# Second and third weight loads cut in halves by rows over two DMA queues in a one-core decoder layer

## The chip, the cores and the metric

The kernel runs on one core of one Trainium2 chip. The metric is device time of one launch in microseconds (us), where lower is better. Before the change the median of three runs is 292.22 us (291.61 to 293.05).

## The reference

One decoder layer on a single sequence of 256 tokens with 1024 features. One input projection feeds three groups of heads: block-sparse causal attention (with 256 tokens there is one block, so it is plain causal attention with a relative bias), a gated width-3 convolution, and a pooling mixer. Their outputs are joined, projected, and added to the input ahead of a layer norm; a gated MLP with a width-3 convolution and a second layer norm follow.

```python
h = x @ w_in
q, k, v, cb, cc, cx, pin = split(h)
attn = causal_attention(q, k, v, rel_bias)
conv = cb * causal_dwconv(cc * cx, conv_w)
pool = pool_mixer(pin, w_pool, pool_scale)
mix = concat([attn, conv, pool]) @ w_out
x = layer_norm(alpha * x + mix, ln1_g, ln1_b)
u, g = split(causal_dwconv(x @ w_up, ffn_conv_w) + ffn_conv_b)
return layer_norm(alpha * x + (u * silu(g)) @ w_down, ln2_g, ln2_b)
```

All inputs and the output are float32.

## The kernel before, in words

**Weights.** All weight matrices are streamed once from HBM through a ring of five buffers named `raw` (`RB = 5`). `load()` (line 96) issues the next loads of the list as long as a buffer is free. The first eight loads are chunks of `a_qk`, one for each block of 128 input features: 128 rows of 1280 float32, that is 256 columns of the transposed input and 1024 columns of the query and key weights, 640 KB in one piece of HBM. Chunks of 1024 KB follow for `a_v`, `a_cp`, `a_out`, `a_up` and `a_down`. Here load 1 is the first chunk, loads 2 and 3 are the second and third. Load 1 comes in two column pieces (lines 106 and 107); all other loads are one DMA each (line 104). All are issued by SyncE (SP), in list order. A load into a buffer that was used before waits until the engines have done with the old content.

**Splitting.** Matmuls run on float32 values split into two float32r numbers. `split` (line 122) takes a raw tile: ScalarE (ACT) writes the high part `hi` (line 123) and VectorE (DVE) writes the remainder `lo` (line 124). For an `a_qk` chunk, `wsplit` (line 130) first splits the 256 input columns into `xh` and `xl`, then the 1024 weight columns into `hi` and `lo`: in three pieces for load 1 (columns 0 to 255 are used unsplit), two for load 2, one for each later load.

**TensorE at the start.** 23 small matmuls on zeros (`WARM`, line 162) run while load 1 is under way. Then come the eight query and key blocks: `qk_block(0)` begins with two matmuls on the raw float32 data (line 200) and continues with 18 split products through `mm3` (line 152); each later `qk_block(k)` has 24 products of 128x256 (line 192), the first 16 of which need `xh`, `xl` and `hi` of load k + 1 and the last 8 `lo`. All eight blocks add into the same four PSUM banks, so they run in order. The value projection, attention, the other mixers, the output projection and the MLP follow, all fed from the same ring.

**Elsewhere.** GpSimd (POOL) issues `prm` and `bias` (lines 176 and 177) once load 4 has landed. ACT issues only output DMAs, at the end. `half` (line 163) is a 128x1 tile of constants that DVE fills at the start; in the kernel before, only GpSimd reads it, in the layer norms.

**Order.** Each engine runs its instructions in program order. The order is written out by hand in `trunk`: `load()` (line 696), the splits of loads 1 and 2, then the blocks with the splits of later loads between them.

Of the kernel before, what the change touches and what calls it, by code (L numbers as in the profile page):

```python
# [10 lines left out]
F32 = mybir.dt.float32  # L11
BF16 = mybir.dt.bfloat16
F32R = mybir.dt.float32r
AF = mybir.ActivationFunctionType
# [3 lines left out]
P = 128  # L18
# [17 lines left out]
LAG = 5  # L36
KEEP = 7
FIRST = 2
WARM = 23


# [16 lines left out]
def trunk(ctx, tc, a_qk, a_v, a_cp, a_out, a_up, a_down, x, par, tab, lnp, out):  # L58
    nc = tc.nc
    cp = ctx.enter_context(tc.tile_pool(name="cp", bufs=1))  # L60
# [6 lines left out]
    def bank():  # L67
        return ps.tile([P, 512], F32, name="bank")
# [14 lines left out]
    for n, i in units:  # L83
        at = {"qk": a_qk, "v": a_v, "cp": a_cp, "out": a_out, "u": a_up, "g": a_up, "d": a_down}[n]
        c = i if n in ("qk", "u", "g") else i // 2
# [3 lines left out]
    for u in units:  # L89
        at, c, _ = src_of[u]  # L90
# [3 lines left out]
    raws, left = [], {}  # L94

    def load():

        while len(raws) < len(loads) and (len(raws) < RB or not left[raws[len(raws) - RB]]):
            at, c = loads[len(raws)]
            key = id(at), c  # L100
            n = S + H if at is a_qk else 2 * H
            raw = raw_of[key] = rp.tile([P, n], F32, name="raw")
            if raws:
                nc.sync.dma_start(raw, at[c])
            else:
                nc.sync.dma_start(raw[:, :2 * S], at[c][:, :2 * S])
                nc.sync.dma_start(raw[:, 2 * S:], at[c][:, 2 * S:])
            raws.append(key)
            left[key] = 1 if at is a_qk else 2
# [7 lines left out]
    def used(u):  # L117
        at, c, _ = src_of[u]
        left[id(at), c] -= 1
        load()  # L120
# [39 lines left out]
    warm = bank()  # L160
    for i in range(WARM):
        nc.tensor.matmul(warm[:, :P], zero, zero, start=True, stop=True)
    half = cp.tile([P, 1], F32, name="half")
# [224 lines left out]
    def sum_rows(accs, rows, last, t, p, lh, ll, h, l, i):  # L388

        ts = slice(t * P, (t + 1) * P)  # L390
        if len(accs[t]) == 0:
            accs[t].extend((bank(), bank()))
        if t == 1 and p == 2 and len(accs[t]) == 2:
            accs[t].append(bank())
        whole = p is None or t == 0
        for b in range(2) if p is None else (p,):
            c, n = (b * 512, 512) if whole else PIECES[t][p]
            o = accs[t][b] if whole else accs[t][p][:, :n]
            mm3(o, lh[:, ts], ll[:, ts], h[:, c:c + n], l[:, c:c + n],
                i == 0 or (t == 1 and p == 2 and i == last), i == rows - 1, skip=True)  # L400
# [16 lines left out]
    def w_out(t, i, p):  # L417
        h, l = W["out", i]
        kt = order[i]
        sum_rows(acc, KD, FIRST, t, p, mh[:, kt], ml[:, kt], h, l, i)  # L420

# [5 lines left out]
    def w_out_last(t, p):  # L427
        for i in range(FIRST, KD):
            w_out(t, i, p)
# [144 lines left out]
    def block(pe, need=(), a=(), b=(), now=False, hold=0, more=True):  # L574
        blocks.append((pe, list(need), list(a), list(b), now, hold, more))
# [60 lines left out]

    for i in range(FIRST):
        block(L(w_out_first, i), [("out", i)])
    last = [("out", i) for i in range(FIRST, KD)]
    block(L(w_out_last, 0, 0), last, [L(rs, 0, 0)], hold=4)  # L640
# [48 lines left out]
    def ready(i):  # L689
# [3 lines left out]
        at, c, _ = src_of[splits[nsplit]]  # L693
        return (id(at), c) in raw_of

    load()
    for _ in range(2):
        wsplit()
# [85 lines left out]
```

## Time and profile before

| | |
|---|---|
| median of three runs | 292.22 us (291.61 to 293.05) |
| profiled execution, its time | 291.71 us |
| profiled execution, its span from first to last instruction | 289.6 us |
| TensorE (PE) matmul busy | 282.8 us, 98% |
| VectorE (DVE) busy | 220.9 us, 76% |
| ScalarE (ACT) busy | 158.4 us, 55% |
| GpSimd (POOL) busy | 40.6 us, 14% |
| moved by DMA | 56.21 MB, mean 194 GB/s |

The time of a run is the span and 2.1 us around it. Busy shares are means over the whole span; TensorE's matmuls overlap one another, so its 98% says that it rarely stands still, not that it runs at its best. Positions in the trace are us from the start of the span. In the trace's tables, an engine name with a q (SPq, ACTq) is that engine's own queue of DMA issues, and DMA queue q1 is the one that SyncE feeds, q0 the one that GpSimd feeds. "Idle before" is how long an engine stood idle ahead of an instruction, and the arrow names what released it. KB is 1024 bytes, MB and GB are decimal.

### The profile page before, as it was taken

What the parts mean: (1) busy time and instruction counts of PE and PEld (TensorE: products, weight loads), DVE (VectorE), ACT (ScalarE), POOL (GpSimd) and SP (SyncE); (2) the same over time, 40 slices, a digit from 0 to 9 for tenths busy, and PEclk for the clock granted to TensorE, in tenths of its full rate; (3) what the DMA queues carried; (4) which work ended last, traced back from release to release, by engine and by line L of the source; (5) the groups of instructions that cost most, each with busy time, mean ns of one, the idle gap of its engine ahead of it and who ended that gap; (6) DMA issues with size and microseconds to landing.
All of it is one profiled execution on the core that took longest, in us unless ns stands there. A gap on an engine that the chain in (4) does not pass through costs nothing.

```text
span 289.6 us, 5052 instructions
## 1 busy us (share of the span) xinstructions
PE 282.8 (98%) x2040; PEld 262.8 (91%) x2040; DVE 220.9 (76%) x384; ACT 158.4 (55%) x263; POOL 40.6 (14%) x42
## 2 busy tenths in 40 slices
PE   8899999999999999999999999999999999999993
PEld 7899779999878999999999999999999999999891
DVE  2774756797958699998988888888667777668584
ACT  3754675828412394366766666666555665655100
POOL 0300004950000289800000000000000000000010
PEclk9999999999999999999999999999999999999998
DMA  6999974143990169284737374848474462200022
GB/s 252 378 354 407 414 272 148 18 145 134 361 359 2 62 231 377 74 285 149 278 147 290 148 285 149 291 148 292 145 290 147 174 224 81 102 2 0 0 76 72
DMA packets 9447, 56.21 MB, mean 194 GB/s; under 512 B 1040, under 2 KB 1552, under 8 KB 3792
## 3 DMA queue, kind: packets, MB, share of 16 engines
q1 hardware_dynamic: 7920, 50.86, 47.1%
q0 software_dynamic: 1072, 4.51, 4.3%
q10 hardware_dynamic: 432, 0.52, 0.5%
q8 instruction: 16, 0.26, 0.4%
q14 instruction: 7, 0.06, 0.1%
HBM read 54.84 MB, written 1.05 MB: 193 GB/s over the span
## 4 chain that ended last, share of the span: by engine, by line
PE 94%; DMA 2%; DVE 1%; ACT 0%; SPq 0%; issue 0%; DVEq 0%
PE bank L152 81%; PE bank L192 7%; PE bank L485 2%; DMA raw<-a_qk 2%; PE bank L267 1%; PE bank L258 1%; PE bank L445 1%; PE bank L227 1%; PE bank L225 0%; DVE xr L565 0%; PE bank L334 0%; DVE xr L560 0%; ACT hi L123 0%; DVE stat L372 0%; DVE xr L385 0%
## 5 line engine op out<-in xcount | busy, mean ns | idle before, releaser
L124 DVE TENSOR_TENSOR lo<-raw,hi 128x1024 fp32r<-128x1024 f32 (+2 forms) x95 | 113.5, 1206 | 24.6 <-ACT hi L123 24.5
L152 PE MATMUL bank<-xh,hi 128*128 128x256 f32 x406 | 114.9, 283 | 0.0
L152 PE MATMUL bank<-xl,hi 128*128 128x256 f32 x406 | 113.6, 280 | 0.0
L152 PE MATMUL bank<-xh,lo 128*128 128x256 f32 x406 | 113.5, 280 | 0.0
L123 ACT ACTIVATE hi<-raw 128x1024 fp32r<-128x1024 f32 (+2 forms) x95 | 95.4, 1019 | 5.2 <-DMA raw<-a_v 4.6
L152 PEld LDWEIGHTS bank<-xh,hi 128*128 128x128 f32 x406 | 76.7, 189 | 1.4 <-issue 0.7
L152 PEld LDWEIGHTS bank<-xl,hi 128*128 128x128 f32 x406 | 76.8, 189 | 0.8
L152 PEld LDWEIGHTS bank<-xh,lo 128*128 128x128 f32 x406 | 76.7, 189 | 0.0
L152 PE MATMUL bank<-hi,mh 128*128 128x512 f32 (+1 forms) x133 | 49.4, 372 | 0.0
L152 PE MATMUL bank<-lo,mh 128*128 128x512 f32 (+1 forms) x133 | 49.2, 370 | 0.0
L152 PE MATMUL bank<-hi,ml 128*128 128x512 f32 (+1 forms) x133 | 49.0, 369 | 0.0
L496 ACT ACTIVATE y<-bank,prm 128x256 f32<-128x256 f32 x44 | 24.6, 560 | 25.8 <-PE bank L152 13.6
L152 PEld LDWEIGHTS bank<-hi,ml 128*128 128x128 f32 x133 | 25.1, 188 | 4.5 <-DVE ml L124 0.2
L410 POOL TENSOR_TENSOR mv<-mv,half 128x1 f32<-128x1 f32 x4 | 2.8, 699 | 186.2 <-DVE mv L409 186.2
L152 PEld LDWEIGHTS bank<-hi,mh 128*128 128x128 f32 x133 | 25.1, 189 | 4.1 <-ACT mh L123 0.4
L152 PEld LDWEIGHTS bank<-lo,mh 128*128 128x128 f32 x133 | 25.1, 188 | 3.5
L497 DVE SCALAR_TENSOR_TENSOR y<-bank,prm,y 128x255 f32<-128x255 f32 x44 | 21.0, 478 | 8.7 <-ACT y L496 8.6
L123 ACT ACTIVATE mh<-f 128x256 fp32r<-128x256 f32 x22 | 9.2, 418 | 24.3 <-DVE f L506 24.3
L498 DVE SCALAR_TENSOR_TENSOR y<-bank,prm,y 128x254 f32<-128x254 f32 x44 | 21.2, 482 | 1.6
L124 DVE TENSOR_TENSOR ml<-f,mh 128x256 fp32r<-128x256 f32 x22 | 11.0, 500 | 10.6 <-ACT mh L123 10.6
L502 ACT ACTIVATE sg<-y 128x256 f32<-128x256 f32 x22 | 9.2, 419 | 13.8 <-DVE y L498 13.8
L192 PE MATMUL bank<-xh,hi 128*128 128x256 f32 x56 | 13.6, 281 | 0.9 <-ACT hi L123 0.9
(105 smaller groups left out, 265.9 us busy)
## 6 DMA issues: line engine op xcount, KB each, us to landing
raw<-a_up SPq DMA_DIRECT2D x22, 1024.0 KB, 4.8
raw<-a_down SPq DMA_DIRECT2D x11, 1024.0 KB, 5.9
raw<-a_qk SPq DMA_DIRECT2D x7, 640.0 KB, 7.8
raw<-a_cp SPq DMA_DIRECT2D x4, 1024.0 KB, 12.7
raw<-a_out SPq DMA_DIRECT2D x4, 1024.0 KB, 4.8
raw<-a_v SPq DMA_DIRECT2D x2, 1024.0 KB, 10.5
lnp<-lnp POOLq DMA_DIRECT2D x4, 512.0 KB, 4.7
bias<-tab POOLq DMA_DIRECT2D x1, 1024.0 KB, 13.3
```

Source lines behind the costliest of these rows:

```text
L123: nc.scalar.activation(hi, raw, AF.Copy)
L124: nc.vector.tensor_sub(lo, raw, hi.bitcast(F32))
L152: nc.tensor.matmul(o, l, r, start=start and i == 0, stop=stop and i == 2, skip_group_check=skip)
L192: nc.tensor.matmul(o, (l if low else h)[:, ws], r[:, k, :], start=False, stop=low and k == KD - 1, skip_group_check=True)
L227: nc.tensor.matmul(s_ps[h][:, P:P + S], qT[r, j, 1], kT[r, j], start=True, stop=True)
L258: nc.tensor.transpose(t_ps[:, i * P:(i + 1) * P], pr[:, i * P:(i + 1) * P], ident)
L267: nc.tensor.matmul(o_ps[s * DH:(s + 1) * DH, t * P:S], v[:, t, h * DH:(h + 1) * DH], pts[h][:, t * S:S + t * P], start=t == 0, stop=t == N ...
L485: nc.tensor.matmul(u_ps[0][:, c:c + P], part(("ug"[s], 0))[:, k * P:(k + 1) * P], xf[:, k, t * P:(t + 1) * P], start=t == 0 and n == 0, st ...
L496: nc.scalar.activation(y, src, AF.Identity, scale=w[2], bias=prm[:, C_FB + c:C_FB + c + 1])
L497: nc.vector.scalar_tensor_tensor(y[:, 1:], src[:, :S - 1], w[1], y[:, 1:], op0=ALU.mult, op1=ALU.add)
L498: nc.vector.scalar_tensor_tensor(y[:, 2:], src[:, :S - 2], w[0], y[:, 2:], op0=ALU.mult, op1=ALU.add)
L502: nc.scalar.activation(ys[j, 2], ys.pop((j, 1)), AF.Silu)
```

## The change

Loads 2 and 3 (`BOTH = 2`) are each issued as two DMAs of 64 rows: rows 0 to 63 by SyncE, rows 64 to 127 by ScalarE. Ahead of the first `load()`, ScalarE runs a new one-column Copy (`first <- half`); the load of the activation table, which stands ahead of the first activation of a program, thereby stands ahead of ScalarE's two DMA issues.

```diff
--- before.py
+++ after.py
@@ -36,6 +36,7 @@
 LAG = 5
 KEEP = 7
 FIRST = 2
+BOTH = 2
 WARM = 23
 
 
@@ -100,7 +101,11 @@
             key = id(at), c
             n = S + H if at is a_qk else 2 * H
             raw = raw_of[key] = rp.tile([P, n], F32, name="raw")
-            if raws:
+            if 0 < len(raws) <= BOTH:
+
+                nc.sync.dma_start(raw[:P // 2], at[c][:P // 2])
+                nc.scalar.dma_start(raw[P // 2:], at[c][P // 2:])
+            elif raws:
                 nc.sync.dma_start(raw, at[c])
             else:
                 nc.sync.dma_start(raw[:, :2 * S], at[c][:, :2 * S])
@@ -693,6 +698,9 @@
         at, c, _ = src_of[splits[nsplit]]
         return (id(at), c) in raw_of
 
+
+    first = cp.tile([P, 1], F32, name="first")
+    nc.scalar.activation(first, half, AF.Copy)
     load()
     for _ in range(2):
         wsplit()
```

Lines of code behind the added ones have higher numbers in the changed program: line 123 becomes 128, 104 becomes 109, 106 becomes 111.

ScalarE's queue from its start, before (`raw_120` is load 1, `raw_123` load 2, `raw_125` load 3, `raw_127` load 4, `raw_129` load 5; a DMAHW semaphore counts a landed DMA):

```order
L123 ACT_TABLE_LOAD
L123 ACTIVATE xh_74<-raw_120 128x256 [waits DMAHW0_49]
L123 ACTIVATE hi_133<-raw_120 128x256 [waits DMAHW1_49]
L123 ACTIVATE hi_133<-raw_120 128x256 x2
L123 ACTIVATE xh_74<-raw_123 128x256 [waits DMAHW2_49]
L123 ACTIVATE hi_143<-raw_123 128x512 x2
L123 ACTIVATE xh_74<-raw_125 128x256 [waits DMAHW3_49]
L123 ACTIVATE hi_178<-raw_125 128x1024
L123 ACTIVATE xh_74<-raw_127 128x256 [waits DMAHW4_49]
L123 ACTIVATE hi_186<-raw_127 128x1024
```

and with the change (`raw_122` is load 1, `raw_125` load 2, `raw_128` load 3, `raw_131` load 4, `raw_133` load 5):

```order
L703 ACT_TABLE_LOAD
L703 ACTIVATE first_120<-half_102 128x1 [waits DVE_49]
L107 DMA raw_125<-a_qk 64x1280
L107 DMA raw_128<-a_qk 64x1280
L128 ACTIVATE xh_74<-raw_122 128x256 [waits DMAHW0_49]
L128 ACTIVATE hi_137<-raw_122 128x256 [waits DMAHW1_49]
L128 ACTIVATE hi_137<-raw_122 128x256 x2
L128 ACTIVATE xh_74<-raw_125 128x256 [waits DMAHW3_49,DMAHW2_49]
L128 ACTIVATE hi_147<-raw_125 128x512 x2
L128 ACTIVATE xh_74<-raw_128 128x256 [waits DMAHW5_49,DMAHW4_49]
L128 ACTIVATE hi_182<-raw_128 128x1024
L128 ACTIVATE xh_74<-raw_131 128x256 [waits DMAHW6_49]
```

The table load keeps its place at the head. The one-column Copy and two DMA issues stand between it and the first split, and the first instruction on load 2, and that on load 3, waits for two landings in place of one.

SyncE's queue from its start, before (names as above; `raw_172` and `raw_174` are loads 6 and 7):

```order
L106 DMA raw_120<-a_qk 128x512
L107 DMA raw_120<-a_qk 128x768
L104 DMA raw_123<-a_qk 128x1280
L104 DMA raw_125<-a_qk 128x1280
L104 DMA raw_127<-a_qk 128x1280
L104 DMA raw_129<-a_qk 128x1280
L104 DMA raw_172<-a_qk 128x1280 [waits DMAHW0_49,DMAHW1_49,DVE_49,PE_49]
L104 DMA raw_174<-a_qk 128x1280 [waits DMAHW2_49,DVE_49]
```

and with the change (`raw_176` and `raw_178` are loads 6 and 7):

```order
L111 DMA raw_122<-a_qk 128x512
L112 DMA raw_122<-a_qk 128x768
L106 DMA raw_125<-a_qk 64x1280
L106 DMA raw_128<-a_qk 64x1280
L109 DMA raw_131<-a_qk 128x1280
L109 DMA raw_133<-a_qk 128x1280
L109 DMA raw_176<-a_qk 128x1280 [waits DMAHW0_49,DMAHW1_49,DVE_49,PE_49]
L109 DMA raw_178<-a_qk 128x1280 [waits DMAHW3_49,DMAHW2_49,DVE_49]
```

SyncE still issues six DMAs ahead of its first wait, in the same places; the third and fourth have 64 rows in place of 128. Loads 4 and 5 stay whole and behind them.

## Rows read from the trace of the kernel before

**Rows 1.** The page: the span, and TensorE's busy time, share and instructions.
```profile
span 289.6 us, 5052 instructions
PE 282.8 (98%) x2040; PEld 262.8 (91%) x2040; DVE 220.9 (76%) x384; ACT 158.4 (55%) x263; POOL 40.6 (14%) x42
```

**Rows 2.** The chain that ended last: start us, us, what.
```profile
1.64 6.70 DMA raw<-a_qk
...
9.35 20.05 PE bank L192 x168
```

**Rows 3.** Timeline of TensorE's matmuls, 3 to 10 us: start us, us, instruction.
```profile
3.55 2.08 PE L200 MATMUL bank<-raw 128*128 128x256 f32 x4
5.07 0.78 PE L152 MATMUL bank<-xh,hi 128*128 128x256 f32 x1
5.64 0.41 PE L152 MATMUL bank<-xl,hi 128*128 128x256 f32 x1
5.85 0.41 PE L152 MATMUL bank<-xh,lo 128*128 128x256 f32 x1
...
6.92 0.36 PE L152 MATMUL bank<-xl,hi 128*128 128x256 f32 x1
...
8.17 0.27 PE L152 MATMUL bank<-xh,lo 128*128 128x256 f32 x1
9.35 0.38 PE L192 MATMUL bank<-xh,hi 128*128 128x256 f32 x1 [0.90 <-ACT hi L123]
9.57 0.28 PE L192 MATMUL bank<-xl,hi 128*128 128x256 f32 x1
```

**Rows 4.** Timeline of ScalarE, 0 to 11 us.
```profile
0.74 1.28 ACT L123 ACT_TABLE_LOAD   x1 [0.74 <-PEq L773]
3.53 0.42 ACT L123 ACTIVATE xh<-raw 128x256 fp32r<-128x256 f32 x1 [1.51 <-DMA raw<-a_qk]
4.49 1.03 ACT L123 ACTIVATE hi<-raw 128x256 fp32r<-128x256 f32 x3 [0.54 <-DMA raw<-a_qk]
8.36 0.42 ACT L123 ACTIVATE xh<-raw 128x256 fp32r<-128x256 f32 x1 [2.84 <-DMA raw<-a_qk]
...
10.30 1.04 ACT L123 ACTIVATE hi<-raw 128x1024 fp32r<-128x1024 f32 x1
```

**Rows 5.** Timeline of SyncE's DMA issues, 0 to 3.6 us.
```profile
0.74 0.37 SPq L106 DMA_DIRECT2D raw<-a_qk  x1
1.17 0.42 SPq L107 DMA_DIRECT2D raw<-a_qk  x1
1.64 1.85 SPq L104 DMA_DIRECT2D raw<-a_qk  x4
```

**Rows 6.** All engines by stretch: A:B us, then busy, PEclk, DMA share, GB/s last.
```profile
0.00:1.74 1.74, 0.75 (x8) 0.75 (x9) 0.12 (x2) 1.00 (x1) 0.20 (x4) 1.00 0.00 0
...
2.50:4.50 2.00, 2.00 (x13) 1.70 (x12) 0.43 (x1) 0.42 (x2) 0.00 (x0) 1.00 0.97 382
4.50:8.35 3.85, 3.85 (x21) 3.50 (x19) 1.09 (x3) 1.02 (x3) 0.00 (x0) 1.00 0.96 355
...
16.00:20.00 4.00, 4.00 (x36) 4.00 (x36) 3.03 (x5) 2.04 (x5) 0.00 (x0) 1.00 0.91 340
20.00:24.00 4.00, 4.00 (x36) 4.00 (x36) 1.45 (x2) 1.01 (x2) 0.00 (x0) 1.00 1.04 399
```

**Rows 7.** DMA from 0 to 8.35 us: packets and bytes moved.
```profile
DMA packets 626, 2.24 MB, mean 268 GB/s; under 512 B 61, under 2 KB 61, under 8 KB 626
```

**Rows 8.** DMA queues from 16 to 20 us: packets, MB, share of 16 engines.
```profile
q0 software_dynamic: 173, 0.69, 48.6%
q1 hardware_dynamic: 111, 0.66, 42.7%
```

**Rows 9.** Groups by line and shape on ScalarE: its shortest; and line 566's DMA issues.
```profile
L240 ACT ACTIVATION_READ_ACCUMULATOR pr<-lg,st 128x1 f32 x16 | 3.0, 188 | 0.0
...
L566 ACTq DMA_DIRECT2D out<-xr x2: 338/338/338, 285.7 to 286.5; - x2
```

## The prediction, made before the changed kernel was run

> **What bounds the kernel now.** I read the page first: TensorE has work under way in 98% of a span of 289.6 us [rows 1], so only a stretch in which it stands still, or runs at its lower clock, has time to give. The chain of waits says where. It is TensorE nearly to its end, but at the start it runs through one transfer: load 2, issued at 1.64 us and 6.70 us under way [rows 2]. From 9.35 us the seven later query and key blocks follow without a gap, 168 matmuls in 20.05 us, 0.119 us each [rows 2].
>
> The timeline of TensorE shows the hole [rows 3]. The last matmul of block 0 starts at 8.17 and, at 0.12 us a matmul, hands over at 8.29. The first of block 1 starts at 9.35. So 1.06 us are lost, and that is all that an earlier load 2 can give back: 0.36% of the run. The profiled run took 291.71 us, 0.51 us below the median of 292.22. About 0.5%, 1.46 us, is what a measurement of this kernel can tell from no change; the three runs lie 0.5% apart. So even the full gain stays below that bound.
>
> ScalarE's timeline shows what the hole waits for: it takes up load 2 at 8.36 [rows 4], and TensorE starts 0.99 us later, after the splits of the input columns and of half the weights. TensorE would be free at 8.29, so load 2 would have to land by 7.3 us to close the hole.
>
> Is load 2 late because it is issued late? No. SyncE issues it at 1.64 us, about 0.47 us after the piece ahead of it, and all six issues are over by 3.49 [rows 5]. The first bytes move at about 1.74 us, 1.0 us after the first issue [rows 5, 6]. From 2.5 us the 16 engines are busy for 0.96 to 0.97 of the time, at 382 and then 355 GB/s [rows 6]. By 8.35 us 2.24 MB have moved [rows 7], while loads 1 and 2 together are 1280 KB, 1.31 MB. So 0.93 MB of later loads came in ahead of load 2's last byte. As SyncE issued them in order, I read this as engines out of step: most are past load 2, and a few that lag hold its last rows. In step it would have been in much sooner: up to 4.5 us 2.24 - 3.85 x 0.355 = 0.87 MB had moved, the missing 0.44 MB take 1.24 us at 355 GB/s, to 5.74. By the same count load 1's 0.66 MB had moved at 3.94, and ScalarE could take its second piece at 4.49 [rows 4], a tail of 0.55 us. With it load 2 would be in at 6.3. The lag is thus about 2.0 us, and issuing from a second queue does not obviously touch it.
>
> **The change part by part.**
>
> *The table load.* It costs nothing: it stays at 0.74 us, for 1.28 us [rows 4], while ScalarE has no input. The number of table loads stays as it is, since the one-column Copy is of the function that the splits use.
>
> *The Copy and the two issues on ScalarE.* The Copy needs `half`, which VectorE writes at the start, while the table loads; it starts at 2.02. Its price lies between nothing and 0.40 us; the nearest row is ScalarE's shortest instruction with 188 ns [rows 9], and I take 0.2. An issue costs 0.34 us on ScalarE's queue at the end [rows 9] and 0.42 to 0.47 on SyncE's at the start [rows 5]; I take 0.45. So load 2's half is issued at 2.2 to 2.3, load 3's at 2.7, and ScalarE is free at 3.1 to 3.3. Its first split starts at 3.53 [rows 4], so 0.2 to 0.4 us of waiting cover all of it. Without that cover the first split would be late by the excess.
>
> *SyncE.* Two issues shrink to half the rows, none goes away: 0.85 us before, between 0.65 and 0.85 us now, all hidden, since the engines have a backlog from 2.5 us on. Loads 4 to 6 are queued behind the same bytes as before, less what travels on the other queue; each needs the sum of all that went ahead, which is the same. GpSimd's issues, which wait for load 4, do not move. Load 6 waits for block 0 and may be issued 0.3 us later, with loads 4 and 5 still queued ahead of it.
>
> *Load 1's second piece.* Here is a cost that the diff does not show. ScalarE's halves, issued at 2.2, are with the engines about 1.0 us later, at 3.25. By then 0.87 - 1.25 x 0.382 = 0.39 MB have moved; of load 1's 0.66 MB 0.27 are missing, all of the second piece, in rows of 3 KB. If the engines take rows of the two queues in turn, each waits for one of 5 KB: 0.44 MB extra, 1.1 us at 382 GB/s. The lower end is nothing, if ScalarE's rows come only behind. I take 0.8, near the upper end: the one stretch with two busy queues, 16 to 20 us, has them moving 0.69 and 0.66 MB side by side [rows 8]. Not all of it is felt. The first split of this piece ends at 4.49 + 0.42 = 4.91 [rows 4], but the matmuls on it flow from 5.42: the second starts at 5.64, at a spacing of 0.21 [rows 3]. So 0.5 us are free and 0.3 show; block 0 ends at 8.3 to 8.6.
>
> *Load 2.* Its halves share the engines with each other, but SyncE's half now also with load 3's half on ScalarE's queue, 0.33 MB that used to come later. That is 0.92 us at 355 GB/s. Does the second queue take the lag away? Two queues together moved 340 GB/s at 16 to 20 us, one alone 399 at 20 to 24 [rows 6], so I see no sign that a second queue adds bandwidth (the GpSimd rows there are shorter, so this is a bound, not a proof). Ends: without any lag load 2 lands at 6.3 + 0.92 = 7.2, just before the 7.3 that closes the hole; change -1.06 to -0.75 us, by whether block 0 is late. With lagging engines that keep their pace over the extra rows (8 rows of load 2 to an engine from 4.49 to 8.34, so four more in 1.9), it lands at 10.2: +1.9 us. Between them lie the full lag, +0.9, and half of it, 8.34 + 0.92 - 1.0 = 8.26, -0.1. I take the middle of these two, **+0.4 us**.
>
> *Load 3.* Its bytes are the sum of all ahead of it, as before. Its split ends at 11.34 [rows 4], and block 2 would start at 9.75 + 2.83 = 12.6. No new wait there.
>
> *Sum.* 0 + 0 + 0.4, with block 0's 0.3 hidden under the later load 2: 291.71 + 0.4 = 292.1 us for the profiled execution. Beside the median of 292.22 that is **292.6 us**: no change that can be told.
>
> **The rivals.**
>
> *The halves change nothing.* The row shows 16 engines already 0.96 busy on one queue [rows 6]; if two queues only share them and the order of bytes is nearly kept, load 2 lands within 0.2 us of 8.34, and the time is 292.0 to 292.4. The Trainium skill speaks against the change in the same way: the page DMA: Bandwidth & Descriptors, section Rules for kernel authors, says of two transfers to disjoint partition halves "Don't bother — they serialize", as both spread over the same 16 engines. By that rule the sum is zero, and no run here has yet tried it. Against this rival: load 3's half moves ahead of a part of load 2.
>
> *The hole closes.* If an engine that is held up on one queue's row goes on with the other's, the lag goes, load 2 lands by 7.3 and the gain is 0.75 to 1.06 us: 291.2 to 291.5. For it: the lag is of single engines, as the 0.93 MB ahead of it show. Against it: the busy share of 0.96 leaves little idle time to fill.
>
> *TensorE falls to its lower clock.* Spacing tells the level: 0.21 us a matmul up to 6.92 us (the 1.2 GHz level), 0.119 later (2.4 GHz) [rows 2, 3]; the granted clock in the table of stretches reads 1.00 in both. The rise came after 5.9 us of unbroken work. The hole of 1.06 us did not undo it: the second matmul of block 1 takes 0.28 us [rows 3]. If load 1's piece is late enough to break the work ahead of the rise, or load 2 comes so late that the hole is much longer than this one, the level may be low again in block 1. Place: blocks 0 and 1. Price: each matmul at the lower level costs 0.09 us more, 2.2 us for a block of 24; with 1 to 1.9 us of waiting that is 3.2 to 4.1 us, 295.4 to 296.3, and less if the low stretch is short. It decides where load 2 lands after some 9.3 us, which doubles the hole. Against it: block 0 feels only 0.3 us.
>
> *The change doesn't do what it says.* If ScalarE's issues come after 3.5 us, its halves land last and also push the first split back by as much. That is a slower run, by 0.5 to 1.5 us, within the range.
>
> **How the numbers follow.** Forecast (load 2 lands between 8.2 and 10.2): 0.42. Nothing changes: 0.18. The hole closes: 0.25. Lower clock: 0.12. Late issues: 0.03. Slower by over 1.46 us needs most of the clock case (0.11) or the far end of the forecast (0.05): 0.16. Faster by over 1.46 us is more than the hole holds; 0.04 is left for the scatter of the runs. Within: 0.80. The range goes from the full gain, 292.22 - 1.06, rounded down to 291.0, to the upper end of load 2, 292.22 + 1.9 = 294.1; it leaves out most of the clock case and some scatter.
>
> **What would show it.** Right: ScalarE's two issues between 2.2 and 3.2 us and its first split still at 3.5; the split of load 1's second piece at about 5.3 in place of 4.49; ScalarE takes up load 2 at about 8.8, and block 1 starts at about 9.75; from there 0.119 us a matmul and the same distance to the end. Wrong: load 2 taken up by 7.5 (the hole closes), a second piece that is not late, a block 1 with a spacing of 0.21, or a difference that arises after 32 us, where I see no effect.

## The result, and the profile after

The changed kernel took **299.25 us** (median; 298.59 to 301.05) against 292.22 for the kernel before: a ratio of **1.0265, interval 1.0237 to 1.0293**, so 7.0 us slower by the medians and 7.7 by the ratio. The forecast was 292.6 us, in a range of 291.0 to 294.1. The profiled execution is the fastest of the changed kernel's five, 298.59 us with a span of 296.4; its account below is thus of the smallest loss that was seen.

The page of after: span, and TensorE's busy time, share and instructions.

```profile
span 296.4 us, 5057 instructions
PE 288.7 (97%) x2040; PEld 267.0 (90%) x2040; DVE 221.3 (75%) x384; ACT 159.1 (54%) x264; POOL 40.0 (14%) x42
```

The number of matmuls is unchanged, and they are busy for 288.7 us instead of 282.8 [rows 1]. Of 6.8 us more span, 5.9 are TensorE working longer on the same work, not waiting longer. The chain of after (start us, us, what) and then a row of the chain of before that wasn't shown yet say where:

```profile
1.65 8.04 DMA raw<-a_qk
...
9.78 0.42 ACT xh L128
...
10.77 21.08 PE bank L197 x168
...
107.23 182.34 PE bank L157 x1293
```

```profile
104.48 178.21 PE bank L152 x1293
```

The account, with [rows 2] for the before:

| Stretch | before | after | difference |
|---|---|---|---|
| block 1 opens at | 9.35 | 10.77 | +1.42 |
| 168 matmuls of blocks 1 to 7 | 20.05 | 21.08 | +1.03 |
| from their end to the last 1293 | 75.08 | 75.38 | +0.30 |
| last 1293 matmuls | 178.21 | 182.34 | +4.13 |

These make 6.9 of the 6.8 us; the tail is 0.1 us shorter. So there are two losses. One is at the start. The other, which is the larger, lies from 107 us on, where loads 2 and 3 have been in for some 95 us: every matmul is a little slower there.

**The late loss.** Timelines of TensorE, some 115 us into the span (start us, duration us, instruction), of before and then of after:

```profile
115.53 0.28 PE L152 MATMUL bank<-xh,hi 128*128 128x256 f32 x1
...
116.58 0.28 PE L152 MATMUL bank<-xh,hi 128*128 128x256 f32 x1
```

```profile
115.34 0.28 PE L157 MATMUL bank<-xh,hi 128*128 128x256 f32 x1
...
116.42 0.28 PE L157 MATMUL bank<-xh,hi 128*128 128x256 f32 x1
```

Both pairs are nine matmuls apart: 1.05 us before, 1.08 after, that is 0.1167 and 0.120 us each. The view of one source line from 108 to 282 us shows it in the durations (min/median/max ns, first and last start), before and after:

```profile
L152 PEld LDWEIGHTS bank<-xl,hi x326: 187/188/189, 107.8 to 264.2; 128*128 128x128 f32 x163
L152 PE MATMUL bank<-xl,hi x326: 277/279/280, 107.9 to 264.3; 128*128 128x256 f32 x163
```

```profile
L157 PE MATMUL bank<-xl,hi x334: 278/283/283, 107.9 to 271.0; 128*128 128x256 f32 x167
...
L157 PEld LDWEIGHTS bank<-xl,hi x333: 187/192/192, 108.1 to 270.8; 128*128 128x128 f32 x167
```

Weight loads take 192 ns in place of 188, matmuls 283 in place of 279, and nothing waits. The clock is not it: in the page's row of 40 slices the granted clock is 0.9 or more in every one but the second.

**The start.** ScalarE's timeline of after, then SyncE's:

```profile
0.74 1.28 ACT L703 ACT_TABLE_LOAD   x1 [0.74 <-PEq L781]
1.00 1.22 ACTq L107 DMA_DIRECT2D raw<-a_qk  x2
2.03 0.20 ACT L703 ACTIVATE first<-half 128x1 f32<-128x1 f32 x1
3.77 0.42 ACT L128 ACTIVATE xh<-raw 128x256 fp32r<-128x256 f32 x1 [1.53 <-DMA raw<-a_qk]
6.80 1.03 ACT L128 ACTIVATE hi<-raw 128x256 fp32r<-128x256 f32 x3 [2.62 <-DMA raw<-a_qk]
9.78 0.42 ACT L128 ACTIVATE xh<-raw 128x256 fp32r<-128x256 f32 x1 [1.95 <-DMA raw<-a_qk]
```

```profile
1.18 0.41 SPq L112 DMA_DIRECT2D raw<-a_qk  x1
1.65 1.50 SPq L106 DMA_DIRECT2D raw<-a_qk  x2
```

The table load starts at 0.74, as before [rows 4], and the Copy at 2.03. But ScalarE's two issues start at **1.00** and 1.6 us, beside the table load and ahead of the Copy that stands before them in its program. The first comes before SyncE's issue of load 1's second piece (1.18), and both before that of load 2's own half (1.65). From 2 to 4 us 0.28 of the 0.52 MB that moved came over ScalarE's queue. That second piece is taken up at 6.80 in place of 4.49, load 2 at 9.78 in place of 8.36 [rows 4]. TensorE's timeline of after shows both, and its clock:

```profile
3.79 1.94 PE L205 MATMUL bank<-raw 128*128 128x256 f32 x4 [0.16 <-DMA raw<-a_qk]
7.27 0.39 PE L157 MATMUL bank<-xh,hi 128*128 128x256 f32 x1 [1.54 <-ACT hi L128]
...
10.77 0.58 PE L197 MATMUL bank<-xh,hi 128*128 128x256 f32 x1 [0.17 <-ACT hi L128]
...
11.36 0.41 PE L197 MATMUL bank<-xh,hi 128*128 128x256 f32 x1
...
12.00 0.41 PE L197 MATMUL bank<-xl,hi 128*128 128x256 f32 x1
```

It waits 1.54 us for load 1's second piece, where before it worked without a break from 3.55 to 8.17 [rows 3]. Stretches of after (A:B us, then length, PE busy (matmuls), granted clock, DMA share, GB/s), and one of before:

```profile
7.00:10.00 3.00, 2.73 (x17) 0.81 1.02 230
...
8.80:12.20 3.40, 3.23 (x16) 0.51 0.99 288
```

```profile
7.00:10.00 3.00, 2.10 (x17) 1.00 0.99 379
```

Two things are to be seen. The DMA engines are as busy as before, but from 7 to 10 us they move 230 GB/s in place of 379: what is under way goes at 0.6 of its pace. And from 8.80 to 12.20 us the granted clock is 0.51, the 1.2 GHz level. Block 1 begins in that stretch: about seven of its matmuls are 0.213 us apart (0.64 us for three, from 11.36 to 12.00) and not 0.118, which costs some 7 x 0.095 = 0.67 us.

So 1.42 + 0.67 = 2.1 us are the start's, and 4.13 + 0.30 and the remaining 0.36 of blocks 1 to 7 = 4.8 us the slower matmuls'.

### The profile page after: what moved, and what is told of

It is laid out like the page before. It is cut to its first block, busy times and chain, and to the rows that moved or that the text cites. A ratio compares the mean times of both kernels' runs of the same rounds, so it can differ in the third digit from the quotient of the medians.

```text
span 296.4 us, 5057 instructions
## 1 busy us (share of the span) xinstructions
PE 288.7 (97%) x2040; PEld 267.0 (90%) x2040; DVE 221.3 (75%) x384; ACT 159.1 (54%) x264; POOL 40.0 (14%) x42
## 3 DMA queue, kind: packets, MB, share of 16 engines
q10 hardware_dynamic: 592, 1.18, 1.3%
HBM read 54.84 MB, written 1.05 MB: 189 GB/s over the span
## 4 chain that ended last, share of the span: by engine, by line
PE 94%; DMA 3%; DVE 1%; ACT 0%; SPq 0%; issue 0%; DVEq 0%; ACTq 0%
PE bank L157 81%; PE bank L197 7%; DMA raw<-a_qk 3%; PE bank L490 2%; PE bank L272 1%; PE bank L263 1%; PE bank L450 1%; PE bank L232 1%; PE bank L230 0%; DVE xr L570 0%; PE bank L339 0%; DVE xr L565 0%; ACT hi L128 0%; DVE stat L377 0%; DVE xr L390 0%
## 5 line engine op out<-in xcount | busy, mean ns | idle before, releaser
L157 PE MATMUL bank<-xh,hi 128*128 128x256 f32 x406 | 116.0, 286 | 1.5 <-ACT hi L128 1.5
L157 PE MATMUL bank<-xh,lo 128*128 128x256 f32 x406 | 115.2, 284 | 0.0
L157 PE MATMUL bank<-xl,hi 128*128 128x256 f32 x406 | 115.0, 283 | 0.0
L157 PEld LDWEIGHTS bank<-xh,hi 128*128 128x128 f32 x406 | 77.9, 192 | 3.6 <-ACT hi L128 2.1
L157 PEld LDWEIGHTS bank<-xl,hi 128*128 128x128 f32 x406 | 78.0, 192 | 0.8
L157 PEld LDWEIGHTS bank<-xh,lo 128*128 128x128 f32 x406 | 78.0, 192 | 0.2 <-DVE lo L129 0.2
L197 PE MATMUL bank<-xh,hi 128*128 128x256 f32 x56 | 14.5, 294 | 0.2 <-ACT hi L128 0.2
```

What stands on the lines that cost most here:

```text
L157: nc.tensor.matmul(o, l, r, start=start and i == 0, stop=stop and i == 2, skip_group_check=skip)
L197: nc.tensor.matmul(o, (l if low else h)[:, ws], r[:, k, :], start=False, stop=low and k == KD - 1, skip_group_check=True)
```

## The experiments

The theory of the late loss was **place**: the change adds a tile, `first`, to the constants' pool `cp`. It is 4 bytes to a partition and takes 32, so every tile allocated after it (the weight splits `hi` and `lo`, `raw`, `xr`) moves by 32 bytes, and those before it, as the input split `xh`, stay. The rivals were the Copy itself, or something that the loads leave behind. All ratios are to the kernel before on the same chip, whose medians were 291.6 to 291.8 us. A ratio is not always that of the two medians; losses in us that follow a ratio go by it.

**e1, the tile and the Copy alone.** All loads whole on SyncE again:

```diff
-BOTH = 2
+BOTH = 0
```

> The kernel before with the new tile and its one-column Copy alone; all loads whole and on SyncE. The new tile moves every buffer behind the constants' pool, hi, lo and raw among them, by 32 bytes. Theory (place): most of the loss has nothing to do with the loads; the products on xh go from 0.117 to 0.120 us each, and the time is 4 to 5.5 us above the kernel before, some 296.5 to 297.5, with block 1 still opening at 9.3 to 9.4 us. Rival (loads): the whole loss comes from the halves and the clock that falls behind them; then this run is at 292.2, within 0.5.

Measured: 296.69 us, ratio 1.0143 (1.0109 to 1.0178). Its chain has the slow matmuls, and its ScalarE takes load 2 up even earlier than before:

```profile
104.59 182.33 PE bank L157 x1293
```

```profile
7.80 0.42 ACT L128 ACTIVATE xh<-raw 128x256 fp32r<-128x256 f32 x1 [2.30 <-DMA raw<-a_qk]
```

With no load changed, 4.2 us of the loss are there by the ratio, and 5.0 by the medians. In its profile block 1 opens at 8.78, 0.57 us earlier than before, and the span is 4.2 us longer: 4.8 us, as in the account above. The loads leave nothing behind; it is the tile or the Copy.

That earlier load 2 is a warning as well. Six of the profiled kernels (before, e1, and e5, e8, e9 and e11 below) have their loads whole and on SyncE. ScalarE takes load 2 up between 7.80 and 8.51 us in them, and block 1 opens between 8.78 and 9.50. Differences of that size at the start say nothing about a change.

**e2, the halves and the Copy, no new tile.** The Copy writes a spare column beside `half`, in the same 32 bytes:

```diff
-    half = cp.tile([P, 1], F32, name="half")
+    halves2 = cp.tile([P, 2], F32, name="halves2")
+    half, first = halves2[:, :1], halves2[:, 1:]
...
-    first = cp.tile([P, 1], F32, name="first")
```

> The changed kernel, but the Copy writes a spare column beside half, in the 32 bytes that half takes anyway, so that no buffer moves. Halves and queues are as changed. Theory (place): the products are back at 0.117 us, and what is left is the late start alone: 2 to 2.5 us above the kernel before, some 294.2 to 294.8, load 1's second piece still taken up near 6.8 us and block 1 opened near 10.8. Rival (loads): as slow as the changed kernel, near 299.2.

Measured: 294.48 us, ratio 1.0083 (1.0053 to 1.0113), so 2.4 us for the start alone. The last 1293 matmuls are back at 178.20 us with the Copy still there: it is the tile's bytes. e1 and e2 add up to 2.26%, against 2.65 measured for both. Its profiled execution was its slowest, and it has the latest start of all profiles here:

```profile
8.99 1.03 ACT L128 ACTIVATE hi<-raw 128x256 fp32r<-128x256 f32 x3 [4.97 <-DMA raw<-a_qk]
```

Load 1's second piece came 4.5 us late there, and block 1 opened at 13.70. How late it comes varies: 2.31 us in the profile of the changed kernel, 2.52 in that of e3, 4.50 here.

**e3, a tile of 64 bytes.** My guess was that 64 bytes would be a whole step and give the pace back:

```diff
-    first = cp.tile([P, 1], F32, name="first")
-    nc.scalar.activation(first, half, AF.Copy)
+    first = cp.tile([P, 16], F32, name="first")
+    nc.scalar.activation(first[:, :1], half, AF.Copy)
```

> The changed kernel with the new tile 64 bytes wide instead of 4: the buffers behind it move by 64 bytes instead of 32, and the Copy still writes one column of it. Theory (place modulo 64 bytes): as without a new tile, 294.2 to 294.8, products at 0.117 us. Rival (any move, or the tile itself, costs): as slow as the changed kernel, near 299.2, products at 0.120.

A miss: 296.06 us, ratio 1.0123 (1.0086 to 1.016). The last 1293 matmuls take 179.68 us, between the two. It is place still, but not in steps of 64 bytes.

**e8 and e5, moving tiles without the change.** If it is how the operands lie to each other, moving all of them alike costs nothing, and moving only a part costs as much as the change. Both are the kernel before with a pad of 4 bytes (32 taken), in e8 ahead of `xh`, in e5 only behind it:

```diff
+    pad = cp.tile([P, 1], F32, name="pad")
+    nc.vector.memset(pad, 0.0)
```

> The kernel before with a new 4-byte tile ahead of all others of the constants' pool: xh, xl, prm, mh, ml, hi, lo and raw all move by 32 bytes, so hi stands at a multiple of 128 bytes as in the changed kernel, but in the same place relative to xh and mh as in the kernel before. Theory (relative place of the two operands of a matmul): nothing changes, 291.7 within 0.5%, 0.117 us a product on xh. Rival (hi's own place): as with the tile and the Copy alone, 296 to 297, 0.120 us.

> The kernel before with a new 4-byte tile just ahead of half: prm, mh, ml, hi, lo and raw move by 32 bytes, xh and xl stay. Theory (relative place): xh and hi stand as in the changed kernel (0 bytes apart modulo 128), so the products on xh take 0.120 us; mh and hi stand as in the kernel before (0 apart), so the 512-column products of the down projection stay at 0.228 us in place of 0.233. Time 3.5 to 4.5 us above before, 295 to 296. Rival (hi's own place): the down products at 0.233 us as well, 296.5 to 297.

Measured: e8 291.64 us, ratio 0.9993 (0.9972 to 1.0013); e5 295.08 us, ratio 1.0116 (1.0077 to 1.0155). The last rows of TensorE in their chains, e8 and e5:

```profile
104.59 178.21 PE bank L152 x1293
```

```profile
106.41 181.42 PE bank L152 x1293
```

Four bytes at one place cost nothing, at another over 1%, with no new Copy and no changed load. Of e5's 3.4 us 3.2 are in these matmuls; it also had a stretch at the lower clock at 11 to 14 us (shown at the end). So the late loss comes from where the tiles lie, and it is the distance between them, not their own place.

**e9 and e11, looking for a good distance.** A pad of 96 bytes at the end of the pool (e9) or ahead of `mh`, the split that the down products read (e11):

```diff
+    pad = cp.tile([P, 24], F32, name="pad")
+    nc.vector.memset(pad[:, :1], 0.0)
```

> The kernel before with a new tile of 96 bytes at the end of the constants' pool: hi, lo and raw move by 96 bytes, xh and mh stay. Of the four places of hi relative to xh modulo 128 bytes this is the one not yet seen (96 is that of before, 0.1167 us a product; 0 that of the changed kernel, 0.1198; 32 gave 0.1184; this is 64). Theory (relative place): some value of its own between 0.113 and 0.120 us, so a time between 288 and 296; if the two operands are best 64 bytes apart it is below the kernel before. Rival (only even or odd multiples of 32 bytes count): 0.1198 us as with a shift of 32, 296 to 297.

> The kernel before with a 96-byte tile ahead of prm: mh and ml move by 96 bytes together with hi, lo and raw; xh and hi are 64 bytes apart, mh and hi 0. Loads as before. Theory (relative place): products on xh at 0.1137 us, as with the 96-byte tile at the pool's end, and 512-column down products at 0.228 us, as in the kernel before: about 1.5 us below that run, 288 to 289.5, a ratio of 0.985 to 0.993. Rival (the gain of 64 bytes apart was paid elsewhere, and is again): 290 to 292.

e9: 290.31 us, ratio **0.995 (0.9927 to 0.9972)**, the fastest of this study, faster than both kernels. e11: 291.29 us, ratio 0.998 (0.9959 to 1.0), a miss against the 288 to 289.5 expected and inside its rival's 290 to 292. The source line's view of one product group, at 108 to 130 and at 150 to 270 us, e9 and then e11:

```profile
L152 PE MATMUL bank<-xl,hi x63: 281/281/281, 108.0 to 129.9; 128*128 128x256 f32 x63
...
L152 PE MATMUL bank<-xl,hi x224: 276/276/281, 152.7 to 263.9; 128*128 128x256 f32 x112
```

```profile
L152 PE MATMUL bank<-xl,hi x66: 276/276/276, 107.7 to 129.8; 128*128 128x256 f32 x66
...
L152 PE MATMUL bank<-xl,hi x224: 281/281/281, 152.0 to 264.8; 128*128 128x256 f32 x112
```

With 64 bytes between the operands there are two paces, and e11, which should have had the better one throughout, has it only where e9 has the worse. Why is open. A part of the gain is lost on the way, too: TensorE stands idle for 1.11 us from 81.49 in e9, and for 1.18 us from 81.86 in e11, until ScalarE has written the last part of `mh` for the output projection. In the kernel before the two came together there, with 0.02 us of waiting. The table puts the runs side by side: start bytes of the tiles modulo 128, as the programs place them, and the time between starts of two matmuls. The 128 is a choice and was not tested: from product to product of one run the operands' distance changes by multiples of 512 bytes, and the pace hardly does, so 256 or 512 would fit as well.

| | xh | mh | hi | on xh, 256 columns, us | on mh, 512 columns, us | last 1293, us |
|---|---|---|---|---|---|---|
| before, e2 | 0 | 96 | 96 | 0.1167 | 0.227 to 0.229 | 178.2 |
| e8 | 32 | 0 | 0 | 0.1167 | 0.228 | 178.21 |
| after, e1 | 0 | 96 | 0 | 0.1198 | 0.233 | 182.34, 182.33 |
| e5 | 0 | 0 | 0 | 0.1198 to 0.120 | 0.227 to 0.229 | 181.42 |
| e3 | 0 | 96 | 32 | 0.1184 | 0.226 to 0.231 | 179.68 |
| e9 | 0 | 96 | 64 | 0.1135 to 0.1178 | 0.232 to 0.236 | 177.48 |
| e11 | 0 | 64 | 64 | 0.1134 to 0.1178 | 0.227 | 177.80 |

Products on `xh` are slowest where both operands start at the same byte modulo 128; those on `mh`, twice as wide, keep their fast pace throughout there. So it is the pair's distance, but no one distance is best for both, and at 64 bytes something else has a say.

**e4, the halves held back.** Now the start. Theory: ScalarE's issues come too early, because nothing holds them. Rival: halves of 64 rows move slowly whenever they are issued. Here the Copy writes into load 2's own buffer, so the issue must wait for it (and there is no new tile):

```diff
+                if len(raws) == 1:
+                    nc.scalar.activation(raw[P // 2:, :1], half[P // 2:], AF.Copy)
...
-    first = cp.tile([P, 1], F32, name="first")
-    nc.scalar.activation(first, half, AF.Copy)
```

> Halves on two queues, no new tile, and ScalarE's first issue held back for real: the one-column Copy writes into the rows that this DMA then overwrites, so the issue waits for the Copy's end. Theory: in the changed kernel nothing held the issues back, they ran beside the table load from 1.0 us; here they come at 2.3 us or later, load 1's second piece is taken up at 4.9 to 5.6 us instead of 6.8, TensorE's clock does not fall, block 1 opens between 9.3 and 10.4, and the time is 292.0 to 293.5. Rival (a second queue is slow by itself, whenever it is issued): load 1's second piece is near 6.8 us again and the time above 294.

Measured: 293.71 us, ratio 1.0057 (1.0034 to 1.0079). ScalarE's timeline and two stretches:

```profile
2.26 1.19 ACTq L109 DMA_DIRECT2D raw<-a_qk  x2
...
4.47 1.03 ACT L130 ACTIVATE hi<-raw 128x256 fp32r<-128x256 f32 x3 [0.51 <-DMA raw<-a_qk]
8.64 0.42 ACT L130 ACTIVATE xh<-raw 128x256 fp32r<-128x256 f32 x1 [3.13 <-DMA raw<-a_qk]
```

```profile
7.00:10.00 3.00, 0.92 (x8) 1.00 1.00 256
...
11.00:15.00 4.00, 4.00 (x23) 0.57 1.02 417
```

Both are at work. Held, the issues start at 2.26, and load 1's second piece is on time again. But from 7 to 10 us the rate is still 256 GB/s, and the clock falls afterwards, which I had not expected. 1.7 us remain, a little more than the theory allowed (292.0 to 293.5). Load 2 is hardly the reason: 8.64 is 0.1 us outside what whole loads show. Load 3 is taken up at 11.16, against 9.97 before, and the chain of waits that ended last runs through it; e6 shows this with the clock at its upper level.

**e6, the halves on one queue.** Before, with the four halves on SyncE:

```diff
+            if 0 < len(raws) <= 2:
+                nc.sync.dma_start(raw[:P // 2], at[c][:P // 2])
+                nc.sync.dma_start(raw[P // 2:], at[c][P // 2:])
...
```

> The kernel before with loads 2 and 3 in halves by rows, all four on SyncE's queue, nothing on ScalarE's and no new tile. Theory (a transfer of 64 rows moves at half rate, on whatever queue): while the four halves are under way, from about 4 to 10 us, some 200 to 210 GB/s move in place of 350 to 390; load 1 is as early as before (second piece taken up near 4.5 us), load 2 lands at 7.5 to 8.5, load 3 near 11 in place of 9.97, and the time is 291.5 to 293.5. Rival (it is the two queues in turn that are slow, not the halves): 350 GB/s and more throughout, load 3 near 10.

**e10, two queues without halves.** e2 with load 3 whole on ScalarE, all others whole on SyncE:

```diff
-            if 0 < len(raws) <= BOTH:
-                nc.sync.dma_start(raw[:P // 2], at[c][:P // 2])
-                nc.scalar.dma_start(raw[P // 2:], at[c][P // 2:])
+            if len(raws) == 2:
+                nc.scalar.dma_start(raw, at[c])
```

> Two queues without halves: load 3 whole on ScalarE's queue, load 2 and all others whole on SyncE's; the Copy writes the spare column beside half, so no buffer moves, and ScalarE's issue runs beside the table load from 1.0 us. Theory (half rate comes from 64 rows): the two queues together move 350 GB/s or more from 2.5 us on; load 1's second piece is late by what of load 3 goes between, taken up at 5.0 to 6.0 us, and load 2 at 8.0 to 9.0; time 292 to 293.5. Rival (two queues in turn are slow): 200 to 300 GB/s as in the changed kernel, and load 1's second piece near 6.8 or later.

Measured: e6 293.63 us, ratio 1.0055 (1.0022 to 1.0088); e10 292.84 us, ratio 1.0031 (1.0013 to 1.0048). Their stretches, e6 and then e10:

```profile
4.00:7.00 3.00, 3.00 (x19) 1.00 0.95 242
7.00:10.00 3.00, 1.16 (x10) 1.00 1.02 222
```

```profile
7.00:10.00 3.00, 3.00 (x17) 1.00 1.01 420
```

This tells the two apart. Halves are slow on one queue too, at 222 to 242 GB/s, and whole loads on two queues move 420. That is no more than one queue can: the six kernels with whole loads on SyncE move 372 to 418 in the same stretch. So the low rate comes from the 64 rows, not from the queues. It is not that the DMAs are smaller, either: load 1's pieces, 256 and 384 KB with all 128 rows, are most of what moved at 382 GB/s from 2.5 to 4.5 us [rows 6], and a half has 320 KB.

What e6 loses, it does not lose at load 2, which is taken up at 8.43; block 1 opens at 9.42, 0.07 us later than before. Load 3 is taken up at 11.24 and not at 9.97. Two rows of e6's chain, the landing of load 3's second half and a later one, and then one of before's:

```profile
3.51 7.65 DMA raw<-a_qk
...
84.30 9.17 PE bank L155 x39
```

```profile
82.13 9.16 PE bank L152 x39
```

From load 3 on the chain runs through ScalarE, VectorE and later loads, until the product of the output projection that needs the last part of `mh` starts at 84.30 in place of 82.13, after TensorE has stood idle for 1.19 us. These 2.17 us are all of the 2.1 by which e6's span is longer. The other runs fit: where load 3 is taken up at 9.6 to 10.0 us and TensorE waits for that part of `mh` (e8, e9, e11), the product starts at 82.2 to 83.0; in e4, and in e12 and e13 below, with load 3 at 11.2 to 11.3, at 83.9 to 84.4. That is read from traces; no run moves load 3 alone. In the changed kernel TensorE itself is late by then and does not wait.

e10 still loses, and its trace shows where:

```profile
1.00 0.38 ACTq L105 DMA_DIRECT2D raw<-a_qk  x1
...
6.04 1.03 ACT L126 ACTIVATE hi<-raw 128x256 fp32r<-128x256 f32 x3 [2.05 <-DMA raw<-a_qk]
7.81 0.42 ACT L126 ACTIVATE xh<-raw 128x256 fp32r<-128x256 f32 x1 [0.74 <-DMA raw<-a_qk]
```

Load 2 comes at 7.81, as early as in e1, but load 1's second piece 1.55 us later than before, since load 3's bytes go ahead of it: 0.45 of the 0.64 MB that moved from 2 to 4 us came over ScalarE's queue. Block 0 ends late, and block 1 opens at 10.35.

**e12, halves by columns, held.** All 128 rows in each half, issued as in e4:

```diff
+            if 0 < len(raws) <= 2:
+                m = n // 2
+                if len(raws) == 1:
+                    nc.scalar.activation(raw[:, m:m + 1], half, AF.Copy)
+                nc.sync.dma_start(raw[:, :m], at[c][:, :m])
+                nc.scalar.dma_start(raw[:, m:], at[c][:, m:])
...
```

> Loads 2 and 3 in halves by columns: two DMAs of 128 rows by 640 columns, on SyncE's and ScalarE's queues, ScalarE's held behind the Copy by its target as in the held run; no new tile. Theory (64 rows is what halves the rate): 350 GB/s or more from 4 to 10 us; load 1's second piece taken up at 4.5 to 5.5 us, load 2 at 7.5 to 9.0, load 3 near 10; time 291.2 to 293. Rival (halves on two queues are slow however they are cut): 200 to 300 GB/s, and a time of 293.5 or more, as the held run by rows.

Measured: 293.13 us, ratio 1.0037 (1.0016 to 1.0059). Its stretches:

```profile
4.00:7.00 3.00, 3.00 (x17) 1.00 0.86 277
7.00:10.00 3.00, 1.18 (x10) 1.00 1.03 407
```

From 7 to 10 us the rate is 407 GB/s against e4's 256, while SyncE's queue already moves whole loads beside ScalarE's halves. But the stretch before gave only 277, not the 350 expected and no more than e4's 275, and why is open. Load 2 is late, taken up for its weights at 8.93, and so is load 3, whose weights are taken up at 11.33. The time misses its 291.2 to 293 by a little, and by the time alone e4 and e12 can't be told apart.

**e13, the best of both.** e11 with load 3 whole on ScalarE, held by a Copy into its own buffer:

```diff
+            if len(raws) == 2:
+                nc.scalar.activation(raw[:, :1], half, AF.Copy)
+                nc.scalar.dma_start(raw, at[c])
...
```

> The 96-byte tile ahead of prm together with load 3 whole on ScalarE's queue, held behind the Copy by its target. Theory: two queues with whole loads moved over 400 GB/s from 4 us on, so held back from load 1 they bring load 2 in at 7.3 to 8.3 us; up to 0.8 us below the run with the tile alone. Rival (load 3 takes bandwidth from load 2, as I forecast for the halves): load 2 at 9 us or later, and 0.5 to 1 us above it.

Measured: 292.92 us, ratio 1.001 (0.9979 to 1.0041), and e11 without the second queue was at 0.998 (0.9959 to 1.0); the two intervals overlap. Load 2 is taken up at 8.82, against 8.44 in e11 and 8.51 at the latest with whole loads on one queue. So the theory's 7.3 to 8.3 is refuted, and the rival, that load 3 takes its share from load 2, is favoured without being reached (9 us or later). From 11 to 14 us the granted clock is 0.56 here.

## Why the prediction was wrong

**The Copy: the step that failed most.** "I take 0.2" priced an instruction. Its 0.20 us at 2.03 are right to the digit, and they are hidden. What was not priced is its output: a tile in the pool that the matmuls' operands stand behind. That term stood at nothing, without a reason. Some 70% of the loss, 4.8 of 6.9 us, come from those 32 bytes. The sign of error was named in advance, "a difference that arises after 32 us, where I see no effect", and it is what came.

**ScalarE's issues: wrong.** "So load 2's half is issued at 2.2 to 2.3" took a queue's order for the order in which its DMAs start. They start at 1.00 and 1.6 and wait for neither the table load nor the Copy, and each takes 0.58 to 0.61 us where I took 0.45. e4 shows what the forecast described: with a true dependency they start at 2.26. My rival that the change doesn't do what it says had the wrong side: the issues came too early, not after 3.5 us.

**Load 1's second piece: right mechanism, wrong size.** That ScalarE's rows go ahead of it was the cost "that the diff does not show". I took 0.8 us late and 0.3 felt, from an issue at 2.2. From 1.00 it is 2.31 us late and TensorE stands for 1.54.

**Load 2: wrong in its rate.** "That is 0.92 us at 355 GB/s" priced the halves at the pace of whole loads. They go at 222 to 256 GB/s (e6, e4). The take-up at 9.78 is 1.42 later than before, inside the bounds of -1.06 and +1.9, but the value of +0.4 in their middle was not. The rule that I weighed as a rival, that such halves only serialize, gave a zero as I read it, and the runs refute that: e4 and e6 lose 1.6 to 1.7 us. Another page bears on it. The Trainium skill, SBUF — State Buffer, section "Door 1: The DMA port swizzle", says that partitions 0 to 63 reach only 8 of the 16 ports and gives 196 GB/s for them against 328 for all 128, each at 1 MiB. The trace agrees in the proportion, with 222 GB/s in halves (e6) and 379 in whole loads (before) from 7 to 10 us; both rates are higher than the page's.

**Load 3: wrong, and hidden.** "No new wait there" counted bytes at one pace. With halves it is taken up at 11.16 to 11.37 (e4, e6, after) in place of 9.97, and e6's longest chain begins with it.

**The lower clock: a rival that came, at a smaller price.** It had two conditions, and the first was met: load 1's piece broke TensorE's work for 1.54 us, and the granted clock fell at 8.80 us, in block 0, ahead of a load 2 that was late as well. The low stretch took in some seven matmuls of block 1 and not 24, so with the 1.42 us of waiting its 0.67 makes 2.1, not the 3.2 to 4.1 of that rival.

**SyncE's issues: wrong, without a visible price.** Half the rows did not make them shorter: two took 1.50 us, where 0.65 to 0.85 was forecast and two whole ones had taken 0.85. The DMA engines stayed busy meanwhile, so no loss is seen there.

**Right.** No version of the loads on two queues beat the kernel before, and the table load cost nothing. That 1.06 us was the most to be had holds for the one execution that I read: in the five other profiles with whole loads on SyncE TensorE stands idle for 1.2 to 2.1 us ahead of block 1, and for 0.9 in this one.

## What to carry to other kernels

A new tile is part of a change's price, however small: before any theory about queues, compare the durations of the same matmuls far from the change, and put a small output into a gap of a tile that exists. Don't split a load by rows: halves of 64 rows moved at 222 to 256 GB/s here, and halves by columns, although faster for a part of the way, gained nothing either. Don't expect the order of one engine's program to hold back its DMA issues: here only data that they depend on did. And follow a late load to the end of the chain: load 3's was felt some 70 us later. Where one load is awaited, a second queue gives the bytes behind it a way past it.

## What I had not expected of the hardware

- The distance of a matmul's two operands in SBUF changes its pace: 0.1134 to 0.120 us for the same 128 x 256 product, and 0.227 to 0.236 for 512 columns. That 64 bytes give two paces within one execution stays open, and so does the mechanism.
- A DMA issue on ScalarE's queue started at 1.00 us, during a table load that ran from 0.74 to 2.02.
- An issue of 64 rows took 0.54 to 0.77 us (after, e4, e6), one of 128 rows 0.37 to 0.45, in halves by columns too (before, e12). Whole issues right behind those of 64 rows took up to 0.85 (e4).
- A DMA busy share of 1.02 stood beside 222 GB/s in e6 and 420 in e10 at 1.01: the share does not tell the rate.
- Like holes had unlike ends. In e5 and e12 TensorE had nothing to do from 8.00 to 9.50 us, and from 11 to 14 us the granted clock was 0.50 in the one and 1.00 in the other. Their whole holes were 2.00 and 1.82 us long. The length alone does not decide it: after 2.07 us in e9 the clock stayed at 1.00, and after 1.54 us in the changed kernel it fell. When it falls was not settled here.

```profile
8.00:9.50 1.50, 0.00 (x0) 1.00 1.01 413
11.00:14.00 3.00, 3.00 (x16) 0.50 0.88 294
```

```profile
8.00:9.50 1.50, 0.00 (x0) 1.00 1.02 408
...
11.00:14.00 3.00, 3.00 (x28) 1.00 0.92 333
```
